# First chunk of an in-projection: its x sums and weight differences formed by VectorE instead of GpSimd

## The chip, the cores and the metric

The kernel runs on one core of a Trainium2 chip. The metric is the device time of one execution in microseconds, as the median of several runs. The engines are TensorE (PE in the profile, its weight loads PEld), VectorE (DVE), ScalarE (ACT), GpSimd (POOL) and SyncE (SP), which here only issues DMAs.

## The reference

One layer of a bidirectional encoder, float32, for 1024 tokens of width 1024: two kinds of attention side by side, then a gated MLP with a short convolution. Only its first matmul, the in-projection, matters here.

```python
hn = rms_norm(x, norm1_g)
proj = hn @ w_in                 # (1024, 1024) @ (1024, 2304) -> qA | kA | vA | qB | kB | vB
...
x = x + mixed @ w_out            # mixed: the two attentions, normed
x = x + conv_ffn(rms_norm(x, norm2_g), w_up, conv_w, conv_b, w_down)
```

## The kernel before

All data of a core lie in two arenas, `bigf` (float32) and `bigr` (float32r, operands of matmuls), and PSUM is one tile `ps` of eight banks of 512 columns. A float32 operand is split into a high half, rounded to float32r by ScalarE, and a low half, the difference, by VectorE; every product is three matmuls: high by high, high by low, low by high.

**The in-projection.** The 256 columns of kA and vA come first, by plain products (`kv_proj`, L292 to L294). The other 2048 columns are taken in four chunks of 512. Per chunk a 2x2 block scheme needs seven products instead of eight. The blocks are the two halves of the tokens, of the width and of the chunk's columns; a product is numbered n, and the first chunk (c = 0) has the order 1, 2, 5, 7, 6, 3, 4. Each product is 48 matmuls of 128x256 (`in_product`, L426 to L428: high by high, high by low, low by high). Its operands are blocks, or sums and differences of blocks:

- of x: `x_sums(tt)` forms four combinations for one of four 128-row slices of x. L258 makes the one of n=5, L259 of n=7, L260 of n=6 (from L258's), L261 of n=3 (from L260's), all in place, 128x512. `s_split(n, t)` then splits them (L246 on ScalarE, L247 on VectorE). These combinations are formed once and serve all chunks.
- of the weights, per chunk and in place, 128x1024: `w_prep(m)`, with L399 for n=5, L401 for n=7, L403 for n=6, L405 for n=4, and the split by L409 (ScalarE) and L410 (VectorE) into one of three buffers. In chunks 1 to 3 all four are on VectorE; in chunk 0 L401, L403 and L405 are on GpSimd.

`in_out` takes finished products from PSUM: L441 copies n=1, L445 n=2, L443 n=5, L449 n=7, and L438 is any add of the scheme, two of which (in chunk 0, at n=6) are on GpSimd. n=6 goes into the PSUM banks that n=5 had, so L443 must have emptied them; n=7 goes into the banks of the last two `kv_proj`.

**Work in between.** The norm's sums of squares are taken on the way: `n_load` (L264) loads a tile of 128 rows of x into one of two buffers, `n_sq` (L267) squares it on ScalarE with a sum, and frees the buffer for the load after next. There are eight such tiles, 0 to 7. `kv_out` (L304, ScalarE) copies a result of `kv_proj` out of PSUM, and L305 sends it to the scratch tensor `kvscr`. The weights of chunk 1 (L379) go into the place of these buffers once tile 7 is squared; L385 scales them.

**What sets the order.** Each engine runs its instructions in order, waiting on semaphores. A scheduler orders them from the program and its dependencies, so moving an instruction to another engine also changes the order of others. The program is emitted twice (`emit(True)`, and a general variant behind a branch that is not taken here); all of this is about the first. All DMAs named here go through SP's queue.

Of the kernel before, what the change touches and what calls it, by code (L numbers as in the profile page):

```python
# [15 lines left out]
OP = mybir.AluOpType  # L16
# [120 lines left out]
def tile_encoder_layer(ctx, tc, x, xT, w_in, w_kv, gains, norm1_g, norm2_g, w_out, w_up, convs,  # L137
# [14 lines left out]
    def emit(bounded):  # L152

        act = nc.scalar.activation
        vec = nc.vector
        gp = nc.gpsimd
# [3 lines left out]
        def f(off, n):  # L160
            return bigf[:, off:off + n]
# [11 lines left out]
        def fp(off, *dims):  # L173
            return raw_ap(bigf[:, off:off + 1], dims)

        def rp(off, *dims):
            return raw_ap(bigr[:, off:off + 1], dims)

        def rfp(off, *dims):
            return raw_ap(bigr[:, off:off + 1].bitcast(F32), dims)  # L180
# [43 lines left out]
        def qab(tt):  # L224
            return O_QAB + 1024 * tt
# [30 lines left out]
        def x_sums(tt):  # L256
            q0, q1 = qab(tt), qab(tt + 4)
            vec.tensor_tensor(f(q1 + 512, 512), f(q1, 512), f(q1 + 512, 512), op=OP.add)  # L258
            vec.tensor_tensor(f(q1, 512), f(q0, 512), f(q1, 512), op=OP.subtract)  # L259
            gp.tensor_tensor(f(q0, 512), f(q1 + 512, 512), f(q0, 512), op=OP.subtract)  # L260
            gp.tensor_tensor(f(q0 + 512, 512), f(q0 + 512, 512), f(q0, 512), op=OP.subtract)  # L261

        def n_load(tt):
            dma(f(F_XN[tt % 2], 1024), perm_rows(x, tt, D))  # L264
# [110 lines left out]
        def w_buf(c, half):  # L375
            return F_WC if half else F_WA[c % 2]
# [12 lines left out]
        def w_op(m):  # L389
            return R_WR + 2048 * (m % 3)  # L390

        def w_prep(m):
            if m >= len(prods):
                return
            c, n = prods[m]
            b11, b12, b21, b22 = [fp(w_buf(c, half) + 256 * u, [512, 4], [1, 256]) for half in range(2) for u in range(2)]
            eng = vec if c else gp
            if n == 5:
                vec.tensor_tensor(b11, b12, b11, op=OP.subtract)  # L399
            elif n == 7:  # L400
                eng.tensor_tensor(b12, b22, b12, op=OP.subtract)  # L401
            elif n == 6:
                eng.tensor_tensor(b11, b22, b11, op=OP.subtract)  # L403
            elif n == 4:
                eng.tensor_tensor(b11, b21, b11, op=OP.subtract)  # L405
            src = {2: b21, 3: b22, 7: b12}.get(n, b11)
            o = w_op(m)
            h = rp(o, [256, 4], [1, 256])
            act(h, src, AF.Copy)  # L409
            vec.tensor_tensor(rp(o + 1024, [256, 4], [1, 256]), src, rfp(o, [256, 4], [1, 256]), op=OP.subtract)  # L410
# [770 lines left out]
        for i in range(4):  # L1181
            kv_proj(i)
            x_prep(i + 2)
            if i == 0:
                late_consts()
            kv_out(i)
            if i == 2:
                w_scale(0, 0)
                w_prep(0)
            if i == 3:  # L1190
                w_scale(0, 1)
                w_prep(1)
        v, rt = f(SM_T + 96, 8), f(SM_MC + 8, 8)
        for m in range(len(prods)):
            c, n = prods[m]
# [8 lines left out]
            if m < 2:  # L1204
                for i in (4 + 2 * m, 5 + 2 * m):
                    kv_proj(i)
                    if i < 6:
                        x_prep(i + 2)
                    x_sums(i - 4)
                    s_split(5, i - 4)  # L1210
                    kv_out(i)
# [18 lines left out]
            if m % 7 == 0 and c > 0:  # L1230
                w_scale(c, 1)
            w_prep(m + 2)
            if m in (7, 16):
                w_load(c + 1, 0)
# [704 lines left out]
```

## Time and profile before

| | us |
|---|---|
| median of 3 runs | 1210.24 (1210.22 to 1210.34) |
| the profiled execution | 1210.31 |
| its span in the profile | 1208.5 |
| busy: TensorE, VectorE, ScalarE, GpSimd | 1179.9, 1009.2, 663.1, 367.3 |

The span is the time from the first to the last recorded work; the profiled execution is 1.8 us longer. The mean granted clock of TensorE is 0.995 of full speed. A row of a timeline reads: start, duration, engine, line, operation, what it writes and reads, how many in a row, and in brackets the idle time of the engine before it and what ended that. In a table of stretches stand, behind the stretch and its length, the busy time of PE, PEld, DVE, ACT and POOL with counts, then the granted clock, the DMA share and GB/s.

### The profile page before, as it was taken

What the parts mean: (1) busy time and instruction counts of PE and PEld (TensorE: products, weight loads), DVE (VectorE), ACT (ScalarE), POOL (GpSimd) and SP (SyncE); (2) the same over time, 40 slices, a digit from 0 to 9 for tenths busy, and PEclk for the clock granted to TensorE, in tenths of its full rate; (3) what the DMA queues carried; (4) which work ended last, traced back from release to release, by engine and by line L of the source; (5) the groups of instructions that cost most, each with busy time, mean ns of one, the idle gap of its engine ahead of it and who ended that gap; (6) DMA issues with size and microseconds to landing.
All of it is one profiled execution on the core that took longest, in us unless ns stands there. A gap on an engine that the chain in (4) does not pass through costs nothing.

```text
span 1208.5 us, 17594 instructions
## 1 busy us (share of the span) xinstructions
PE 1179.9 (98%) x6548; PEld 1001.0 (83%) x6548; DVE 1009.2 (84%) x1353; ACT 663.1 (55%) x964; POOL 367.3 (30%) x247
## 2 busy tenths in 40 slices
PE   7799999999999999999999999999999999999998
PEld 7799999666668998888788888888888888888886
DVE  6768687889988888666999999999999997966673
ACT  6575545889887777435553534435344453543331
POOL 2810122230004440010355656556565523000000
PEclk9899999999999999999999999999999999999999
DMA  8245311020005556223222332323332257967872
GB/s 319 84 148 140 88 53 43 1 54 22 1 17 126 126 132 200 88 93 107 63 76 96 108 116 94 105 96 114 102 108 105 96 191 269 353 216 249 294 231 79
DMA packets 118779, 151.20 MB, mean 125 GB/s; under 512 B 51361, under 2 KB 78753, under 8 KB 117665
## 3 DMA queue, kind: packets, MB, share of 16 engines
q1 hardware_dynamic: 116544, 144.27, 37.0%
q0 software_dynamic: 2144, 5.77, 2.1%
q8 instruction: 52, 0.85, 0.3%
q14 instruction: 39, 0.31, 0.1%
HBM read 111.47 MB, written 33.82 MB: 120 GB/s over the span
## 4 chain that ended last, share of the span: by engine, by line
PE 84%; DMA 4%; DVE 4%; ACT 3%; POOL 2%; issue 2%; SPq 0%; ACTq 0%; POOLq 0%
PE ps L1575 11%; PE ps L1573 11%; PE ps L1574 11%; PE ps L735 6%; PE ps L1716 6%; PE ps L1715 6%; PE ps L1717 6%; PE ps L964 3%; PE ps L999 2%; PE ps L1104 2%; PE ps L1106 2%; PE ps L1105 2%; PE ps L751 2%; PE ps L752 2%; PE ps L426 2%
## 5 line engine op out<-in xcount | busy, mean ns | idle before, releaser
L1573 PE MATMUL ps<-bigr 128*128 128x512 f32 x616 | 239.8, 390 | 0.5 <-ACT bigr L1158 0.5
L1574 PE MATMUL ps<-bigr 128*128 128x512 f32 x616 | 239.6, 389 | 0.0
L1575 PE MATMUL ps<-bigr 128*128 128x512 f32 x616 | 239.6, 389 | 0.0
L1612 DVE SCALAR_TENSOR_TENSOR bigf<-bigf 128x768 f32<-128x768 f32 (+1 forms) x176 | 193.3, 1134 | 0.7
L1541 ACT ACTIVATE bigr<-bigf 128x512 fp32r<-128x512 f32 x154 | 91.7, 622 | 141.7 <-POOL bigf L1533 109.1
L1695 ACT ACTIVATE bigr<-bigf 128x1024 fp32r<-128x1024 f32 (+1 forms) x99 | 83.6, 867 | 115.7 <-PE ps L1717 69.3
L426 PE MATMUL ps<-bigr 128*128 128x256 f32 x448 | 128.2, 286 | 8.8 <-ACT bigr L246 7.5
L1573 PEld LDWEIGHTS ps<-bigr 128*128 128x128 f32 x616 | 115.6, 188 | 24.7 <-ACT bigr L1158 0.9
L1574 PEld LDWEIGHTS ps<-bigr 128*128 128x128 f32 x616 | 115.6, 188 | 24.1
L1575 PEld LDWEIGHTS ps<-bigr 128*128 128x128 f32 x616 | 115.6, 188 | 24.0
L427 PE MATMUL ps<-bigr 128*128 128x256 f32 x448 | 127.7, 285 | 1.3 <-DVE bigr L410 1.3
L428 PE MATMUL ps<-bigr 128*128 128x256 f32 x448 | 127.7, 285 | 1.0 <-DVE bigr L247 1.0
L1715 PE MATMUL ps<-bigr 128*128 128x512 f32 x308 | 119.8, 389 | 0.0
L1716 PE MATMUL ps<-bigr 128*128 128x512 f32 x308 | 119.8, 389 | 0.0
L1696 DVE TENSOR_TENSOR bigr<-bigf,bigr 128x1024 fp32r<-128x1024 f32 (+1 forms) x99 | 96.6, 995 | 27.8 <-ACT bigr L1695 22.8
L1717 PE MATMUL ps<-bigr 128*128 128x512 f32 x308 | 119.8, 389 | 0.0
L1542 DVE TENSOR_TENSOR bigr<-bigf,bigr 128x512 fp32r<-128x512 f32 x112 | 105.9, 948 | 3.0 <-ACT bigr L1541 2.3
L735 PE MATMUL ps<-bigr 128*66 128x512 f32 x384 | 99.8, 394 | 0.0
L426 PEld LDWEIGHTS ps<-bigr 128*128 128x128 f32 x448 | 86.9, 194 | 9.4 <-ACT bigr L246 7.7
L427 PEld LDWEIGHTS ps<-bigr 128*128 128x128 f32 x448 | 86.9, 194 | 1.5 <-DVE bigr L410 1.5
L428 PEld LDWEIGHTS ps<-bigr 128*128 128x128 f32 x448 | 86.7, 194 | 1.3 <-DVE bigr L247 1.3
L762 DVE TENSOR_TENSOR bigr<-bigf,bigr 128x1024 fp32r<-128x1024 f32 x64 | 80.7, 1268 | 6.4 <-ACT bigr L761 5.7
(221 smaller groups left out, 2475.7 us busy)
## 6 DMA issues: line engine op xcount, KB each, us to landing
bigf<-w_down SPq DMA_DIRECT2D x99, 256.0 KB, 4.1
bigf<-w_up SPq DMA_DIRECT2D x44, 512.0 KB, 3.5
bigf<-gscr SPq DMA_DIRECT2D x77, 256.0 KB, 4.3
gscr<-bigf SPq DMA_DIRECT2D x31, 512.0 KB, 2.6
bigf<-w_in SPq DMA_DIRECT2D x8, 1024.0 KB, 5.6
bigf<-x SPq DMA_DIRECT2D x16, 512.0 KB, 4.6
bigf<-xT SPq DMA_DIRECT2D x8, 512.0 KB, 7.7
bigf<-w_out SPq DMA_DIRECT2D x8, 512.0 KB, 3.5
```

The lines of the kernel that those rows point to most:

```text
L426: mm(o, ah, wh, start=(k == 0 and t % 2 == 0 and n != 2), stop=False, skip_group_check=True)
L427: mm(o, ah, wl, start=False, stop=False, skip_group_check=True)
L428: mm(o, al, wh, start=False, stop=(k == 3), skip_group_check=True)
L735: mm(bank(ob)[0:66], r(w, 66), r(p + 512 * u, 512), start=(kt == 0 and i == 0), stop=(kt == 7 and i == 2))
L1542: low = lambda eng: eng.tensor_tensor(rp(o + 512, [128, 4], [1, 128]), src, rfp(o, [128, 4], [1, 128]), op=OP.subtract)
L1573: mm(bank(b), wh, th, start=(k == 0 and n in (1, 5, 6, 7)), stop=False, skip_group_check=True)
L1574: mm(bank(b), wh, tl, start=False, stop=False, skip_group_check=True)
L1575: mm(bank(b), wl, th, start=False, stop=(k == 3), skip_group_check=True)
L1612: vec.scalar_tensor_tensor(f(a + o, n), f(i + d, n), w_, f(a + o, n), op0=OP.mult, op1=OP.add)
L1715: mm(o, ah, r(d, 512), start=(q == 0 and n in (1, 5, 2)), stop=False, skip_group_check=True)
L1716: mm(o, ah, r(d + 1024, 512), start=False, stop=False, skip_group_check=True)
L1717: mm(o, al, r(d, 512), start=False, stop=(q == NQ - 1), skip_group_check=True)
```

## The change

In `x_sums` the combinations of n=6 and n=3 (L260, L261), and in `w_prep` the chunk-0 differences L401, L403 and L405, are issued to VectorE instead of GpSimd. Their inputs, outputs and place in the program text stay.

```diff
             vec.tensor_tensor(f(q1, 512), f(q0, 512), f(q1, 512), op=OP.subtract)
-            gp.tensor_tensor(f(q0, 512), f(q1 + 512, 512), f(q0, 512), op=OP.subtract)
-            gp.tensor_tensor(f(q0 + 512, 512), f(q0 + 512, 512), f(q0, 512), op=OP.subtract)
+            vec.tensor_tensor(f(q0, 512), f(q1 + 512, 512), f(q0, 512), op=OP.subtract)
+            vec.tensor_tensor(f(q0 + 512, 512), f(q0 + 512, 512), f(q0, 512), op=OP.subtract)
...
             b11, b12, b21, b22 = [fp(w_buf(c, half) + 256 * u, [512, 4], [1, 256]) for half in range(2) for u in range(2)]
-            eng = vec if c else gp
+            eng = vec
```

Eleven instructions move: four L260, four L261, and one each of L401, L403 and L405. TensorE's order stays; VectorE's, ScalarE's and SP's change between the first products. GpSimd's order around the place, before and then after:

```order
 L387 TENSOR_SCALAR bigf<-bigf 128x512 x2
-L401 TENSOR_TENSOR bigf<-bigf 128x4x256
-L260 TENSOR_TENSOR bigf<-bigf 128x512 x2
-L261 TENSOR_TENSOR bigf<-bigf 128x512 x2
-L403 TENSOR_TENSOR bigf<-bigf 128x4x256
-L260 TENSOR_TENSOR bigf<-bigf 128x512
-L261 TENSOR_TENSOR bigf<-bigf 128x512
-L260 TENSOR_TENSOR bigf<-bigf 128x512
-L261 TENSOR_TENSOR bigf<-bigf 128x512
-L405 TENSOR_TENSOR bigf<-bigf 128x4x256
 L438 TENSOR_TENSOR bigf<-bigf 128x4x256 x2
```

GpSimd's first two-input operation is now L438, at n=6.

VectorE, after, from the last combinations of x to the split of n=6's weights (the first L410 is n=7's weights, the second n=6's; the L247 between them are the four x splits of n=7 and the last of n=6, then three of n=3):

```order
L260 TENSOR_TENSOR bigf<-bigf 128x512
L247 TENSOR_TENSOR bigr<-bigf,bigr 128x512
L261 TENSOR_TENSOR bigf<-bigf 128x512
L401 TENSOR_TENSOR bigf<-bigf 128x4x256
L247 TENSOR_TENSOR bigr<-bigf,bigr 128x512 x3
L410 TENSOR_TENSOR bigr<-bigf,bigr 128x1024
L247 TENSOR_TENSOR bigr<-bigf,bigr 128x512 x5
L403 TENSOR_TENSOR bigf<-bigf 128x4x256
L247 TENSOR_TENSOR bigr<-bigf,bigr 128x512 x3
L410 TENSOR_TENSOR bigr<-bigf,bigr 128x1024
```

Before, twelve L247 and no combination stood behind the L410 of n=7; now all eight moved combinations of x, and the last splits of n=5, stand ahead of it.

ScalarE, before, behind the copy of n=1 (L441); the first L409 is n=7's weights, the second n=6's:

```order
L441 ACTIVATE bigf<-ps 128x1024
L409 ACTIVATE bigr<-bigf 128x1024
L246 ACTIVATE bigr<-bigf 128x512
L304 ACTIVATE bigf<-ps 128x256 x3
L246 ACTIVATE bigr<-bigf 128x512 x2
L267 ACTIVATE ps,bigf<-bigf 128x1024
L246 ACTIVATE bigr<-bigf 128x512
L267 ACTIVATE ps,bigf<-bigf 128x1024
L246 ACTIVATE bigr<-bigf 128x512 x3
L409 ACTIVATE bigr<-bigf 128x1024
```

ScalarE, after, from square 0 to n=7's weights and x splits (of the last L246 rows, three and one are those of n=7):

```order
L267 ACTIVATE ps,bigf<-bigf 128x1024
L246 ACTIVATE bigr<-bigf 128x512 x2
L267 ACTIVATE ps,bigf<-bigf 128x1024
L246 ACTIVATE bigr<-bigf 128x512 x2
L267 ACTIVATE ps,bigf<-bigf 128x1024
L246 ACTIVATE bigr<-bigf 128x512 x2
L267 ACTIVATE ps,bigf<-bigf 128x1024
L304 ACTIVATE bigf<-ps 128x256
L409 ACTIVATE bigr<-bigf 128x1024
L246 ACTIVATE bigr<-bigf 128x512 x3
L304 ACTIVATE bigf<-ps 128x256
L246 ACTIVATE bigr<-bigf 128x512
```

The weights of n=7 stood right behind L441 and now stand behind four squares, of tiles 0 to 3. In both orders L443 stands behind the square of tile 6.

## The prediction, made before the result

> **What bounds the kernel now.** I read the page first, then the waits of TensorE, then a table of stretches, then the timelines of the engines around the one long wait.
>
> ```profile
> PE 1179.9 (98%) x6548; PEld 1001.0 (83%) x6548; DVE 1009.2 (84%) x1353; ACT 663.1 (55%) x964; POOL 367.3 (30%) x247
> ```
>
> TensorE is busy for 1179.9 of the 1208.5 us of the span. So an edit gains only where TensorE stands idle or runs slowly. Its waits over the whole span name the places; these are the ones on ScalarE and VectorE results in the in-projection's products (columns: total us, times, longest):
>
> ```profile
> PE ps L426 <- ACT bigr L246: 7.5, 1, 7.5
> PE ps L428 <- DVE bigr L247: 1.0, 1, 1.0
> PE ps L426 <- ACT bigf L441: 0.7, 1, 0.7
> PE ps L426 <- ACT bigf L443: 0.6, 1, 0.6
> ```
>
> L426 to L428 are the products of the in-projection. The timeline of TensorE puts the first two and the last of these rows in the first chunk, at its products n=7 and n=6:
>
> ```profile
> 44.58 0.28 PE L426 MATMUL ps<-bigr 128*128 128x256 f32 x1
> ...
> 50.22 0.28 PE L428 MATMUL ps<-bigr 128*128 128x256 f32 x1
> 57.98 0.58 PE L426 MATMUL ps<-bigr 128*128 128x256 f32 x1 [7.48 <-ACT bigr L246]
> ...
> 60.17 0.41 PE L426 MATMUL ps<-bigr 128*128 128x256 f32 x1
> ...
> 67.77 0.38 PE L426 MATMUL ps<-bigr 128*128 128x256 f32 x1 [0.55 <-ACT bigf L443]
> ```
>
> Product n=5 runs from 44.58 to its 48th matmul at 50.22, one every 0.12 us, 5.76 us in all; n=7 starts at 57.98, n=6 at 67.77. The table of stretches shows the clock (PEclk, behind the busy times):
>
> ```profile
> 27.00:34.00 7.00, 7.00 (x60) 7.00 (x60) 7.00 (x12) 4.97 (x8) 6.88 (x1) 1.00 0.23 83
> 50.00:55.00 5.00, 0.50 (x5) 0.30 (x3) 4.85 (x4) 2.55 (x4) 4.01 (x3) 0.83 0.00 0
> 55.00:60.00 5.00, 1.00 (x3) 0.71 (x4) 4.01 (x5) 4.98 (x12) 2.74 (x1) 0.50 0.60 181
> ```
>
> Behind the idle time the granted clock is 0.50, so n=7 begins at half speed. The loss in this place is 67.77 - 50.34 = 17.43 us for a product that needs 5.76: 11.67 us. That is the most the edit can recover here.
>
> Why n=7 is late is read from GpSimd and ScalarE:
>
> ```profile
> 27.12 11.40 POOL L401 TENSOR_TENSOR bigf<-bigf 128x1024 f32<-128x1024 f32 x1 [8.74 <-DMA kvscr<-bigf]
> ```
> ```profile
> 38.55 1.06 ACT L409 ACTIVATE bigr<-bigf 128x1024 fp32r<-128x1024 f32 x1 [6.59 <-POOL bigf L401]
> ...
> 49.08 0.63 ACT L246 ACTIVATE bigr<-bigf 128x512 fp32r<-128x512 f32 x1 [4.18 <-POOL bigf L260]
> 52.45 1.15 ACT L246 ACTIVATE bigr<-bigf 128x512 fp32r<-128x512 f32 x2 [2.73 <-POOL bigf L260]
> ```
>
> GpSimd's first difference lasts 11.40 us. ScalarE issues in order and stands 6.59, 4.18 and 2.73 us before results of GpSimd; the splits (L246) that n=7 reads are queued behind those. By 52.45 it has the last of the sums it waits for, and n=7 follows at 57.98.
>
> **The change, part by part.** Eleven GpSimd instructions go to VectorE: eight of 128x512 (L260, L261) and three of 128x1024 (L401, L403, L405). Their price there, and what VectorE's own work costs beside GpSimd: the first row groups VectorE's splits from 26.5 to 36.3 us, the second those from 38.5 to 55.2 us (mean ns behind the bar).
>
> ```profile
> L247 DVE TENSOR_TENSOR bigr<-bigf,bigr 128x512 fp32r<-128x512 f32 x7 | 4.5, 692 | 0.0
> ```
> ```profile
> L247 DVE TENSOR_TENSOR bigr<-bigf,bigr 128x512 fp32r<-128x512 f32 x7 | 10.0, 1472 | 5.7 <-ACT bigr L246 5.6
> ```
> ```profile
> 29.02 0.69 DVE L247 TENSOR_TENSOR bigr<-bigf,bigr 128x512 fp32r<-128x512 f32 x1
> 29.62 1.23 DVE L410 TENSOR_TENSOR bigr<-bigf,bigr 128x1024 fp32r<-128x1024 f32 x1
> 30.75 3.10 DVE L247 TENSOR_TENSOR bigr<-bigf,bigr 128x512 fp32r<-128x512 f32 x5
> ...
> 34.97 1.29 DVE L259 TENSOR_TENSOR bigf<-bigf 128x512 f32<-128x512 f32 x2
> ...
> 55.16 1.21 DVE L410 TENSOR_TENSOR bigr<-bigf,bigr 128x1024 fp32r<-128x1024 f32 x1
> ...
> 84.06 1.23 DVE L401 TENSOR_TENSOR bigf<-bigf 128x1024 f32<-128x1024 f32 x1
> 85.20 1.22 DVE L438 TENSOR_TENSOR bigf<-ps,bigf 128x1024 f32<-128x1024 f32 x1
> ```
>
> From start to start 128x512 costs 0.60 us (29.02 to 29.62) and 128x1024 1.13 us (29.62 to 30.75); L401 on VectorE, in the second chunk, 1.14 (84.06 to 85.20). The edit adds 8 x 0.60 + 3 x 1.14 = 8.2 us to VectorE. It also takes away the slowing: seven splits at 1472 instead of 692 ns give back 5.5 us, and VectorE's idle 5.7 us stands in the same row. So VectorE has room for the added work before 55 us.
>
> Now the walk in the order after. VectorE is the same up to 29.02. From there to the end of the third split of n=6 sums, just ahead of n=7's weight split, it has 23 instructions of 128x512 and 2 of 128x1024: 23 x 0.60 + 2 x 1.13 = 16.1, so 45.1; L401, four rows earlier, is done at 43.3. It does not set the end, because ScalarE's order puts two squares of x (L267, tiles 2 and 3) ahead of that split, and these need loads. Prices for ScalarE and the load:
>
> ```profile
> 28.36 2.70 ACT L246 ACTIVATE bigr<-bigf 128x512 fp32r<-128x512 f32 x5
> ...
> 65.65 1.03 ACT L267 ACTIVATE ps<-bigf 128x1024 f32<-128x1024 f32 x1 [0.74 <-DMA bigf<-x]
> 66.71 1.00 ACT L443 ACTIVATE bigf<-ps 128x1024 f32<-128x1024 f32 x1
> ```
> ```profile
> 60.95 4.62 DMA bigf<-x
> ```
>
> A split is 0.54, a square 1.06, a load 4.62 from the square that frees its buffer; L409 takes about 1.0, an L304 copy is taken as 0.3, half a split.
>
> - ScalarE waits for the second L260 (8 x 0.60 + 1.13 after 29.02: 34.95), then a split, a copy and square 0: 36.9. Load 2 lands at 41.5. Square 2 ends at 42.6, two splits 43.7, square 3 (its buffer was freed later, at about 39.1, so it lands at 43.7) 44.8, copy 45.1, n=7's weights on ScalarE 46.1, on VectorE 47.3. Its first x split is there at 47.9. TensorE wants both at 50.34: 2.4 us in hand, and the 7.5 and 1.0 us waits go. With no idle time the clock keeps 1.00, as from 27 to 34: n=7 takes 5.76 us and ends at 56.10.
> - What is late next is the bank of n=6: L443 must empty it. It is queued behind squares 4, 5 and 6. Three x splits, a copy and the fourth take ScalarE to 48.6, square 4 to 49.7; its buffer's load 6 lands at 54.3. Square 6 and L443 then need, as in the rows before, 67.77 - 65.65 = 2.12 us: n=6 starts at 56.4. TensorE waits 0.3 us there instead of 0.6.
> - The weights of n=6 and n=3: L403 follows the n=7 splits (51.4 done), its ScalarE half 53.3, its VectorE half 54.5, before 56.4. L405 and the n=3 weights come at about 58.5, wanted at 62.2. No wait.
> - No DMA is added. SP's queue has loads 2 to 5 ahead of the two last copies to kvscr instead of one between; those copies are wanted only in the second chunk, so nothing is charged.
>
> Sum: n=6 starts at 56.4 instead of 67.77, 11.37 us earlier; I round to 11.3. From there the engines' orders are as before, and what they wait for moves with them: square 7, which frees the buffer for the next chunk's weights, follows L443 and one weight half in both. The profiled execution took 1210.31 us, of which 1.8 lie outside the span, and the median is 0.07 below it. 1210.31 - 11.3 = 1199.0.
>
> **The rivals.**
>
> (a) The loads of x set the pace. Three trips (loads 2, 4, 6) now lie in a row before L443. Load 4 has 1.3 us to spare (it lands at 47.3, wanted at 48.6). If each takes d longer, n=6 starts 3d - 1.3 us later: with d = 1, 1200.7; with d = 3, 1206.7. For it: the copies to kvscr share the queue. Against: these are loads of 0.5 MB, two at a time, and in the stretch 50 to 55 nothing else moved (last column, 0 GB/s).
>
> (b) GpSimd's 11.40 us is a cost of its first such instruction and only moves on. For it: VectorE's splits ran at 692 ns under that row, while under the others they took 1472, so GpSimd may not have been reading yet. Then the next one pays:
>
> ```profile
> 75.99 5.76 POOL L438 TENSOR_TENSOR bigf<-bigf 128x1024 f32<-128x1024 f32 x2 [16.80 <-DVE bigf L438]
> ```
>
> Moved to 64.7, a first one of 11.40 ends at 76.1; VectorE's add of n=3 (85.20 before, 73.9 then) needs it and is 2.2 us late, with L441's wait of 0.7 us behind a full VectorE: 1201.2. Against: GpSimd's row ends at 38.5, 2.3 us after VectorE's last row before its idle time (34.97 and 1.29), a usual length, as if it had waited for that. [...]
>
> (c) VectorE becomes the bound, and the kernel gets slower. It is full from 27 to 34 us (7.00 of 7.00). If its 1472 ns are its own and not GpSimd's doing, they hold from 38 us on: by then 18 instructions of 128x512 and 4 of 128x1024, 26 units, remain to n=6's weights; 26 x 1.47 = 38.2 puts n=6 at 76.2, 8.4 us later than before: 1218.7. It decides at (67.77 - 38) / 26 = 1.15 us a unit. Against: the row at 55.16, in a gap of GpSimd, has 1.21 for 128x1024, the undisturbed price. [...]
>
> (d) The waits go but something else holds n=7 just as long, within 0.2%: it would take (a) with d near 4.
>
> **How the numbers follow.** The forecast, 1198.4 to 1200.2, has 0.66: its low end is the whole 11.67 us and 0.2 us for the other executions, its high end an extra 1.2 us of ScalarE waiting. (a) beyond that, 1200.2 to 1207.8, has 0.18, (b) 0.11, (c) 0.02, (d) 0.03. The range 1197.9 to 1202.5 takes the forecast, (b) and the near half of (a), and half a microsecond below for a load that lands early. A measurement of this kernel can tell about 0.2%, 2.4 us, from no change: faster 0.95, same 0.03, slower 0.02.
>
> **What would show it.** After: no idle time of TensorE between n=5 and n=7, PEclk 1.00 from 50 to 66 us, n=6 starting at 56 to 57 us behind L443; VectorE's splits at about 692 ns throughout; GpSimd empty from 18 to about 64 us. ScalarE waiting for x at squares 2, 3 and 6 shows the walk, with waits well over the few us written here it shows (a). A long first L438 on GpSimd shows (b), splits at 1472 ns without GpSimd (c). The forecast is wrong if n=6 starts after 60 us, or if the start of the second chunk's first product moves by less than n=6 does.

## The result, and the profile after

| | median us | runs | ratio to before, 95% interval |
|---|---|---|---|
| before | 1210.23 | 4 (1210.16 to 1210.34) | |
| changed | 1198.62 | 4 (1197.84 to 1198.97) | 0.9903 (0.9886 to 0.9920) |
| changed, a second time, beside a before of 1210.76 | 1198.46 | 4 (1197.96 to 1199.66) | 0.9899 (0.9884 to 0.9914) |

The change gains 11.6 us. The page after, its span and busy times:

```profile
span 1197.0 us, 17588 instructions
PE 1178.0 (98%) x6548; PEld 999.8 (84%) x6548; DVE 1009.3 (84%) x1364; ACT 662.8 (55%) x964; POOL 338.9 (28%) x236
```

VectorE has eleven more instructions and 0.1 us more busy time: what came was paid by what was no longer slowed (689 ns a split, where seven of them had taken 1472). TensorE's timeline after, at the last plain product (L294) and the first matmul of n=5, at the first and last of n=7, and at the first of n=6 (each product is 48 matmuls, one every 0.12 us):

```profile
45.05 0.28 PE L294 MATMUL ps<-bigr 128*128 128x256 f32 x1
45.17 0.28 PE L426 MATMUL ps<-bigr 128*128 128x256 f32 x1
...
50.93 0.28 PE L426 MATMUL ps<-bigr 128*128 128x256 f32 x1
...
56.57 0.28 PE L428 MATMUL ps<-bigr 128*128 128x256 f32 x1
56.69 0.28 PE L426 MATMUL ps<-bigr 128*128 128x256 f32 x1
```

No brackets: nothing was waited for. n=6 starts at 56.69 instead of 67.77. The stretches after, and then before in steps of 2 us, for the clock (the third column from the end):

```profile
45.00:50.00 5.00, 5.00 (x44) 5.00 (x44) 3.91 (x6) 5.00 (x12) 0.00 (x0) 1.00 0.56 182
50.00:55.00 5.00, 5.00 (x44) 5.00 (x43) 5.00 (x8) 4.41 (x8) 0.00 (x0) 1.00 0.63 198
55.00:60.00 5.00, 5.00 (x44) 5.00 (x43) 3.40 (x8) 4.97 (x8) 0.00 (x0) 1.00 0.26 57
```
```profile
52.00:54.00 2.00, 0.00 (x0) 0.00 (x0) 1.85 (x2) 1.55 (x3) 1.92 (x2) 0.83 0.00 0
...
62.00:64.00 2.00, 2.00 (x13) 2.00 (x13) 0.00 (x0) 1.88 (x4) 0.00 (x0) 0.61 0.76 227
```

ScalarE after, at the places the forecast walked through:

```profile
41.15 1.03 ACT L267 ACTIVATE ps<-bigf 128x1024 f32<-128x1024 f32 x1 [0.61 <-DMA bigf<-x]
...
44.15 1.03 ACT L267 ACTIVATE ps<-bigf 128x1024 f32<-128x1024 f32 x1 [0.81 <-DMA bigf<-x]
...
53.92 1.03 ACT L267 ACTIVATE ps<-bigf 128x1024 f32<-128x1024 f32 x1 [0.59 <-DMA bigf<-x]
...
54.97 1.01 ACT L443 ACTIVATE bigf<-ps 128x1024 f32<-128x1024 f32 x1
```

Two of VectorE's groups from 26.5 to 55 us, and GpSimd's first two-input instructions after:

```profile
L247 DVE TENSOR_TENSOR bigr<-bigf,bigr 128x512 fp32r<-128x512 f32 x21 | 13.6, 689 | 0.0
L410 DVE TENSOR_TENSOR bigr<-bigf,bigr 128x1024 fp32r<-128x1024 f32 x3 | 3.7, 1224 | 1.1 <-ACT bigr L409 1.1
```
```profile
64.26 5.76 POOL L438 TENSOR_TENSOR bigf<-bigf 128x1024 f32<-128x1024 f32 x2 [45.64 <-DVE bigf L438]
```

### The profile page after: what moved, and what is told of

The parts are those of the page before. It is cut to its first block, busy times and chain, and to the rows that moved or that the text cites. A ratio compares the mean times of both kernels' runs of the same rounds, so it can differ in the third digit from the quotient of the medians.

```text
span 1197.0 us, 17588 instructions
## 1 busy us (share of the span) xinstructions
PE 1178.0 (98%) x6548; PEld 999.8 (84%) x6548; DVE 1009.3 (84%) x1364; ACT 662.8 (55%) x964; POOL 338.9 (28%) x236
## 4 chain that ended last, share of the span: by engine, by line
PE 87%; DVE 3%; ACT 1%; POOL 1%; issue 1%; DMA 0%; ACTq 0%; POOLq 0%; DVEq 0%
PE ps L1575 11%; PE ps L1573 11%; PE ps L1574 11%; PE ps L735 6%; PE ps L1716 6%; PE ps L1715 6%; PE ps L1717 6%; PE ps L426 3%; PE ps L427 3%; PE ps L428 3%; PE ps L964 3%; PE ps L999 2%; PE ps L1106 2%; PE ps L1104 2%; PE ps L1105 2%; PE ps L751 2%
## 5 line engine op out<-in xcount | busy, mean ns | idle before, releaser
L427 PE MATMUL ps<-bigr 128*128 128x256 f32 x448 | 126.9, 283 | 1.4 <-DVE bigr L410 1.4
L427 PEld LDWEIGHTS ps<-bigr 128*128 128x128 f32 x448 | 86.0, 192 | 1.6 <-DVE bigr L410 1.6
```

The lines of the kernel that those rows point to most:

```text
L427: mm(o, ah, wl, start=False, stop=False, skip_group_check=True)
```

## The experiments

Two theories stood. **Held:** a GpSimd instruction that arrives while VectorE runs two-input instructions back to back gets to work only when VectorE falls idle, and afterwards the two take turns, each slowing the other. **First use:** the 11.40 us of L401 were a cost of GpSimd's first such instruction. Beside them, what of the change matters: the sums, the weights, or one instruction.

**The sums alone.** The weight differences stay on GpSimd.

```diff
-            gp.tensor_tensor(f(q0, 512), f(q1 + 512, 512), f(q0, 512), op=OP.subtract)
-            gp.tensor_tensor(f(q0 + 512, 512), f(q0 + 512, 512), f(q0, 512), op=OP.subtract)
+            vec.tensor_tensor(f(q0, 512), f(q1 + 512, 512), f(q0, 512), op=OP.subtract)
+            vec.tensor_tensor(f(q0 + 512, 512), f(q0 + 512, 512), f(q0, 512), op=OP.subtract)
```

> Only the x combinations (L260, L261) go to VectorE; the three weight differences stay on GpSimd. ScalarE's order has n=7's weights (L409) right behind the copy of n=1, so it waits for L401. Theory 'held' (a GpSimd instruction that comes while VectorE runs back to back gets its operands only when VectorE falls idle): VectorE's row of work ends at about 38.2 us, where it needs a split that ScalarE has not made, and L401 ends about 2.3 us later, near 40.6, some 13.5 us long. n=7 then starts near 54, n=6 near 63.6: 1198.6 + 7.3 = 1206. Theory 'first use' (L401's 11.4 us are a cost of its own): L401 ends near 38.5 as before, n=6 near 61.5: 1204. If the weights were all that mattered: 1210, no gain; if the sums were: 1198.6.

Measured: 1204.9 us, ratio 0.9954 (0.9937 to 0.9971). GpSimd's first instruction, and VectorE's last row before its idle time:

```profile
26.96 13.20 POOL L401 TENSOR_TENSOR bigf<-bigf 128x1024 f32<-128x1024 f32 x1 [8.74 <-ACT bigf L385]
```
```profile
37.22 0.69 DVE L259 TENSOR_TENSOR bigf<-bigf 128x512 f32<-128x512 f32 x1
```

L401 lasts longer than before and ends at 40.16, 2.25 us after VectorE fell idle at 37.91. The median lies between the two theories' times and does not tell them apart; the row does: "held" had the end at 40.6, "first use" at 38.5. ScalarE, with n=7's weights first in its order, stood 8.4 us before L401, and its whole queue came late: n=7 waits 1.99 us, and n=6 waits for L443:

```profile
61.80 0.38 PE L426 MATMUL ps<-bigr 128*128 128x256 f32 x1 [1.45 <-ACT bigf L443]
```

**The weights alone.** The sums stay on GpSimd.

```diff
-            eng = vec if c else gp
+            eng = vec
```

> Only the weight differences (L401, L403, L405) go to VectorE; the x combinations stay on GpSimd. Theory 'held': the first L260, ready at about 27.2 us, waits until VectorE falls idle near 37.5 us and ends near 38.8, some 11 us long; the fourth L260 ends near 47.6 instead of 52.4, n=7 starts near 53, n=6 near 63: about 1205. Theory 'first use': the first GpSimd instruction, now L260, lasts 8 to 9 us over its 1.3 whatever VectorE does, so its end is near 37.5 too; the two differ in whether that end follows VectorE's idle time. If the order of the loads of x and not GpSimd set the time: 1210.

Measured: 1209.18 us (1205.88 to 1212.21, 10 runs), ratio 0.9986 (0.9974 to 0.9997): a tenth of the gain, not the nearly half that was expected. The ten fall into two groups, four of 1205.9 to 1206.9 and six of 1209.0 to 1212.2, and the first is near the expected 1205. The first row is as "held" has it:

```profile
29.03 9.91 POOL L260 TENSOR_TENSOR bigf<-bigf 128x512 f32<-128x512 f32 x1 [10.26 <-DMA kvscr<-bigf]
```
```profile
36.50 1.28 DVE L259 TENSOR_TENSOR bigf<-bigf 128x512 f32<-128x512 f32 x2
```

It ends at 38.94, 1.16 us after VectorE (37.78). n=7 starts at 53.73 (expected 53) and, after a second wait and at half clock, n=6 at 63.87 (expected 63). So the first chunk came as expected, and the miss lies behind it, in a stretch of the fourth chunk that the expectation had taken as unchanged; the last two rows have its clock:

```profile
53.73 0.39 PE L426 MATMUL ps<-bigr 128*128 128x256 f32 x1 [2.54 <-ACT bigr L246]
...
55.63 0.58 PE L428 MATMUL ps<-bigr 128*128 128x256 f32 x1 [1.40 <-DVE bigr L247]
...
63.87 0.28 PE L426 MATMUL ps<-bigr 128*128 128x256 f32 x1
```
```profile
56.00:58.00 2.00, 2.00 (x11) 2.00 (x11) 1.39 (x3) 1.13 (x3) 0.00 (x0) 0.50 0.92 297
...
170.00:180.00 10.00, 6.26 (x47) 5.86 (x46) 7.03 (x11) 5.28 (x7) 1.81 (x5) 0.88 0.00 0
180.00:190.00 10.00, 10.00 (x70) 10.00 (x69) 9.47 (x15) 7.33 (x11) 0.00 (x0) 0.77 0.01 2
```

In the fourth chunk TensorE waits 1.66 us for L441 and then 2.08 for L410, where the changed kernel waits once, 1.4 us, at full clock. The profiled execution took 1212.21 us, the slowest of the ten. That this place makes the two groups is likely, but only this one execution was profiled.

**L401 alone.**

```diff
-            eng = vec if c else gp
+            eng = vec if c or n == 7 else gp
```

> Only L401 goes to VectorE. GpSimd's row of work starts with L260 instead, held until VectorE falls idle near 37.5 us, and still has L403 between its sums: the fourth L260 ends near 50.4, n=7 starts near 56 at a lower clock, n=6 near 65.6: about 1208. If L401's 11.4 us were the whole cause, as ScalarE's longest wait (6.6 us) says on its face, removing it would bring n=7 to about 51.4: 1200 or less.

Measured: 1209.4 us, ratio 0.9994 (0.9984 to 1.0004). GpSimd now begins with L403, not with L260 as expected, and that one is held:

```profile
26.75 12.53 POOL L403 TENSOR_TENSOR bigf<-bigf 128x1024 f32<-128x1024 f32 x1 [8.74 <-ACT bigf L385]
```
```profile
35.74 1.28 DVE L259 TENSOR_TENSOR bigf<-bigf 128x512 f32<-128x512 f32 x2
```
```profile
55.51 0.58 PE L426 MATMUL ps<-bigr 128*128 128x256 f32 x1 [5.37 <-ACT bigr L246]
```

It ends at 39.28, 2.26 us after VectorE (37.02), and n=7 still waits 5.37 us. ScalarE's longest wait before (6.6 us for L401) was not a 6.6 us gain: what came first on GpSimd in its place, L403 with 12.53 us, inherited it.

**Load on GpSimd whose results nobody reads.** The changed kernel, with 24 additions.

```diff
+        def busy():
+            o, i = O_F + 5888, fp(O_IDF, [0, 2], [1, 128])
+            gp.tensor_tensor(f(o, 256), f(qab(4) + 512, 256), i, op=OP.add)
+            for _ in range(23):
+                gp.tensor_tensor(f(o, 256), i, i, op=OP.add)
...
                     x_sums(i - 4)
+                    if bounded and i == 4:
+                        busy()
```

> The changed kernel with 24 additions of 128x256 on GpSimd that nobody reads (into a free place), the first one ready when the first x combination of n=5 is, about 27 us. No instruction of the kernel depends on them. Each costs about 0.7 us of GpSimd. Theory 'held': they wait until VectorE's first idle time at 45.5 us, leave VectorE at 0.69 us a split until then, and alternate with it from there on: 11 VectorE instructions to n=6's weights, each about 0.7 us later, so n=6 starts some 6 us late: 1204 to 1205. Theory 'shared' (the two alternate from the first one): VectorE is slowed from 27 us on, n=7's weights come about 17 us late, n=7 starts some 14 us late: 1213 to 1216. If only the dependencies on GpSimd counted and not its traffic: 1198.6.

Measured: 1209.75 us, ratio to before 0.9992 (0.9982 to 1.0002): the whole gain is gone, but not by the additions' traffic alone, as the rows further down show. GpSimd (its lines are numbered six higher here), VectorE's last row ahead of its idle time, and its splits from 26.5 to 45 us and from 45.5 to 66:

```profile
26.60 18.44 POOL L265 TENSOR_TENSOR bigf<-bigf 128x256 f32<-128x256 f32 x1 [9.00 <-DMA kvscr<-bigf]
45.12 23.97 POOL L267 TENSOR_TENSOR bigf<-bigf 128x256 f32<-128x256 f32 x23
```
```profile
42.56 1.88 DVE L247 TENSOR_TENSOR bigr<-bigf,bigr 128x512 fp32r<-128x512 f32 x3
```
```profile
L247 DVE TENSOR_TENSOR bigr<-bigf,bigr 128x512 fp32r<-128x512 f32 x11 | 7.2, 681 | 0.0
```
```profile
L247 DVE TENSOR_TENSOR bigr<-bigf,bigr 128x512 fp32r<-128x512 f32 x9 | 9.4, 1097 | 0.0
```

The first addition stands 18.44 us and ends at 45.04, 0.60 us after VectorE (44.44); until then VectorE is undisturbed at 681 ns, then at 1097. That is "held"; "shared" would have slowed it from 27 us on. The time came 5 us above what "held" had forecast, and that has two parts:

```profile
56.56 0.38 PE L432 MATMUL ps<-bigr 128*128 128x256 f32 x1 [0.93 <-ACT bigf L449]
58.13 0.39 PE L433 MATMUL ps<-bigr 128*128 128x256 f32 x1 [1.19 <-DVE bigr L416]
...
78.46 0.38 PE L432 MATMUL ps<-bigr 128*128 128x256 f32 x1 [1.44 <-ACT bigr L415]
79.72 0.58 PE L433 MATMUL ps<-bigr 128*128 128x256 f32 x1 [0.88 <-DVE bigr L416]
...
95.51 0.39 PE L432 MATMUL ps<-bigr 128*128 128x256 f32 x1 [2.87 <-ACT bigf L447]
```
```profile
SPq L385 <- POOL bigf L267: 10.6, 1, 10.6
```
```profile
74.76 2.56 ACT L391 ACTIVATE bigf<-bigf 128x512 f32<-128x512 f32 x4 [9.88 <-DMA bigf<-w_in]
```

The first two rows are what the traffic did. The splits were slowed by 0.42 us each and not 0.7; n=7 did not wait, n=6 started 1.1 us behind the end of n=7 and then took 8.78 us instead of 5.76. That is some 4 us by the start of n=3, where 6 were expected. The rest is not traffic. The place that the additions write (`O_F + 5888`, 256 columns) is the end of the buffer for the next chunk's weights (`F_WA[1]`, from `O_F + 4096`, 2048 columns), so it was not free: their load (L379, here L385) waits 10.6 us for the last addition and is issued at 69.11 us instead of 57.99. ScalarE stands 9.88 us for it, and the waits at 78 and 95 us follow. Each of the three places also holds some 3.4 us at half speed, an estimate from the granted clock, taken as either 1.00 or 0.50: it is 0.76 from 56 to 63 us, 0.76 from 77 to 84 and 0.72 from 95 to 101. So the rows show "held" and the slowing, but the time does not show what the traffic alone would cost. A load that is put in as an experiment must write where nothing is going to be written.

**GpSimd writes only.** The changed kernel, with 120 memsets of the same place instead of the additions.

```diff
+            for _ in range(120):
+                gp.memset(f(o, 256), 0.0)
```

> The changed kernel with 120 memsets of 128x256 on GpSimd that nobody reads, back to back from about 18 us. They write and read nothing. Theory 'reads' (what holds GpSimd behind VectorE and slows VectorE behind GpSimd is the reading of two inputs): the memsets run at once, the splits stay at 0.69 us, 1198.6. Theory 'any traffic of GpSimd': memsets held until 45 us and VectorE's instructions slowed from there, as with the additions: 1204 to 1210.

Measured: 1199.3 us (1197.95 to 1199.67), ratio to before 0.9901 (0.9886 to 0.9916). Part of the memsets, and VectorE's splits from 26.5 to 55 us beside them:

```profile
22.65 26.62 POOL L266 MEMSET bigf<- 128x256 f32 x72
```
```profile
L247 DVE TENSOR_TENSOR bigr<-bigf,bigr 128x512 fp32r<-128x512 f32 x19 | 12.2, 680 | 0.0
```

72 of them ran at 0.37 us each beside VectorE's full row, held by nothing, and VectorE's splits stayed at 680 ns. The memsets were done by 49.27 us, before the next chunk's weights were loaded. So GpSimd's writing did neither here; what the additions do beside it is read two inputs. Reading one was not tried, nor was VectorE with anything but two-input instructions in its row.

**Without the moved work.** The changed kernel with the eleven instructions left out.

```diff
+            if bounded:
+                return
             vec.tensor_tensor(f(q0, 512), f(q1 + 512, 512), f(q0, 512), op=OP.subtract)
...
+            elif c == 0 and bounded:
+                pass
             elif n == 7:
```

> The changed kernel without the eleven moved instructions on any engine (n=6 and n=3, and the weights of n=7, 6 and 4 of the first chunk, use the operands as they lie): a look at what their 8.2 us on VectorE cost. If they lie wholly beside TensorE's work, as the forecast has it: the same as the changed kernel within 0.5 us. If VectorE's load reached the end: up to 8 us less, 1190.5.

Measured: 1198.96 us (1197.72 to 1199.75), against 1198.46 of the changed kernel on the same chip. VectorE's share of the stretch behind 45 us falls and nothing follows; the first row is the changed kernel, the second this one:

```profile
45.00:55.00 10.00, 10.00 (x85) 10.00 (x85) 8.91 (x13) 9.41 (x19) 0.00 (x0) 1.00 0.59 190
```
```profile
45.00:55.00 10.00, 10.00 (x86) 10.00 (x85) 3.10 (x5) 8.34 (x15) 0.00 (x0) 1.00 0.60 186
```

The work moved to VectorE, 8.2 us by the forecast's prices, lies wholly beside TensorE's.

**The last two adds as well.**

```diff
-                for o, eng in ((c22, vec), (c12, vec if c else gp), (c21, vec if c else gp)):
+                for o, eng in ((c22, vec), (c12, vec), (c21, vec)):
```

> The changed kernel with the two adds L438 that GpSimd still does in the first chunk also on VectorE. They slow one VectorE instruction from 1.2 to 3.4 us in the changed kernel, but TensorE does not wait there. Theory 'only a wait of TensorE pays': the same as the changed kernel within 0.5 us. Theory 'relief of VectorE pays': the 2.2 us of that slow instruction are gained, 1196.4.

> The changed kernel once more, beside the next ones: 1198 to 1199, with n=6 of the first chunk following n=7 without idle time.

Measured: 1200.8 us (1198.76 to 1201.89, 5 runs), ratio to before 0.9909 (0.9896 to 0.9923), the changed kernel beside it 0.9899 (0.9884 to 0.9914). The relief of VectorE paid nothing. The median is 2.3 us above the changed kernel's, more than the half microsecond expected; whether the adds cost that is not settled, since the intervals overlap. The profiled execution, 1201.89, has one longer wait on VectorE in the fourth chunk, 2.1 us where the changed kernel's second profile (1197.96) has 0.7, and behind it a lower clock:

```profile
PE ps L427 <- DVE bigr L410: 2.1, 1, 2.1
```
```profile
PE ps L427 <- DVE bigr L410: 0.7, 1, 0.7
```
```profile
168.00:172.00 4.00, 2.95 (x17) 2.95 (x18) 3.97 (x7) 3.95 (x6) 0.00 (x0) 0.73 0.00 0
172.00:176.00 4.00, 4.00 (x30) 4.00 (x30) 3.93 (x9) 2.75 (x5) 0.00 (x0) 0.84 0.00 0
```

The wait and 3.4 us at half speed, 1.4 + 1.7 us by estimate, are most of the 3.9 us between these two executions. The same wait is 1.8 us in the run with the memsets, whose adds stayed on GpSimd, so the adds need not be its cause.

## Why the prediction was right

1198.6 us came against 1199.0 forecast, in the range. By its steps:

- **The loss to recover, 11.67 us.** From the start of n=5 to that of n=6 it was 67.77 - 44.58 = 23.19 us and is 56.69 - 45.17 = 11.52, two products without a wait. All 11.67 came back.
- **n=7's operands in time.** Forecast: weights on ScalarE 46.1 and on VectorE 47.3. They ended at 46.52 and 47.78, the latter after an idle 1.1 us for L409, as in the walk. What set it was the loads, not L401: squares 2 and 3 waited 0.61 and 0.81 us for x. n=7 wanted them at 50.93.
- **What is late next.** L443 behind square 6 was the right instruction and mis-sized by 0.4 us. Square 6 began at 53.92, not 54.3, and L443 ended at 55.98, 0.7 us before n=6 wanted its bank. The term of 0.3 us is zero. The walk leaves out the copy L445 (1.02 us at 50.33) ahead of square 5; it cost nothing, because square 6 waited 0.59 us for its load behind it.
- **No DVE bound.** Rival (c) needed 1.15 us for 128x512; it stayed at 0.69. The run without the moved work shows that nothing was paid.
- **Rival (b)** is out: the first L438 did not inherit anything. The pair took 5.76 us as before. The argument against (b) in the forecast, the end 2.3 us after VectorE's idle begins, was the cause itself.
- **Rival (a)** did not come: no wait for x was over 0.81 us. The forecast's argument against it, the 0 GB/s from 50 to 55 us before, said nothing either way: no load of x was under way in that stretch.
- **Not forecast:** two things that nearly cancel, so part of the close fit is luck. TensorE reached n=5 at 45.17 instead of 44.58, 0.59 us late, because its slow start lasted longer: a matmul every 0.21 us instead of 0.12, to 13.8 us where it was 12.3 (the clock column shows 1.00 there). And the 0.7 us wait for L441 is gone from this profile; it is 0.5 in the second one of the same kernel. Over the ten profiles here n=5 starts anywhere from 43.95 to 45.27 us, so a walk from one profile can be off by about a microsecond.

## What to carry to other kernels

In these runs a two-input GpSimd instruction that arrived beside a VectorE running two-input instructions without a pause stood 9.9 to 18.4 us and ended only after VectorE stopped, 0.60 to 2.26 us later; beside the ones behind it, VectorE's splits took 1472 ns (before) and 1097 (the load) instead of 692 and 681. So before giving VectorE's elementwise work to GpSimd, look for a GpSimd row that is several times as long as its like (here 11.40 us against 2.85) and ends just after VectorE's idle time begins; if TensorE waits behind it (7.48 us here), the work may be faster on the "full" engine, as here. Do not price such a move by one long wait: here the next GpSimd instruction inherited it (12.53 us), and parts of the change brought between nothing and half of the gain (ratios of 0.9994, 0.9986 and 0.9954, the whole 0.9903).

## What was not expected of the hardware

- **How completely GpSimd was held.** The time from VectorE's idle to the end of the held instruction was at most its length beside an idle VectorE, whatever it had stood before: 2.25 to 2.26 us for 128x1024 (before: 38.52 - 36.26; sums alone; L401 alone), 1.16 for 128x512 (weights alone), 0.60 for 128x256 (the load). With VectorE idle, the same shapes took 2.40 us (L403, sums alone), 1.29 (L261, weights alone) and 0.75 (the median of the four L325, before). The held ones had stood 9.9 to 18.4 us. Behind VectorE's row they show no turn of their own; once one was in, GpSimd and VectorE ran beside each other, both slower (before: splits at 1472 ns on average instead of 692, the single L260 and L261 behind L403 at 1.59 to 2.27 us instead of 1.29). Why the two differ, the runs do not show.
- **How little idle time stood ahead of the half clock.** With the sums alone, the clock went to 0.50 behind waits of 1.99 and 0.42 us with half a microsecond of work between them:

```profile
52.00:54.00 2.00, 1.29 (x5) 1.09 (x6) 2.00 (x4) 2.00 (x6) 0.00 (x0) 0.73 0.76 216
54.00:56.00 2.00, 2.00 (x12) 2.00 (x11) 2.00 (x3) 2.00 (x5) 0.00 (x0) 0.50 0.52 182
56.00:58.00 2.00, 2.00 (x17) 2.00 (x17) 1.90 (x4) 1.65 (x4) 1.76 (x1) 0.91 0.78 246
```

With the clock taken as either 1.00 or 0.50, an estimate, that is half speed for 2 x (0.27 + 0.50 + 0.09) x 2 = 3.4 us. Single waits in the fourth chunk (L427 on L410) of 1.4 us (first profile of the changed kernel) and 1.6 (the load) left the clock at 1.00, and with one of 0.7 (second profile) it was 1.00 on the mean of the whole span; behind 2.1 us with one of 0.2 ahead of it (the last two adds) it was 0.73, and with 2.9 us alone (the load) 0.83 from 90 to 100 us. So in this run two short waits cost more than their sum: n=7 took 7.89 us from 52.29, that is its 5.76, the 0.42 and another 1.7. It did not reach the end, because n=6 then waited 1.45 us for L443 anyway.
